# A hybrid decoder trunk on one core: another order of the weight folding and the x tiles in the prelude, the second block's rotary tables behind the softmax, and the third retention head scaled on the vector engine

## The chip, the cores and the metric

The kernel runs on one core of a Trainium2 chip. A core has a matrix engine (PE, with its weight loads shown as PEld), a vector engine (DVE), a scalar engine (ACT), a general engine (POOL) and an engine that mostly issues DMAs (SP). Each runs its own instructions in order, and waits on semaphores for the others. The metric is the time of one execution in microseconds (us) on the device; lower is better.

## The reference

One layer of a decoder trunk on x of 2048 tokens by 1024 columns, in f32, with 256 memory tokens. Cut to what matters:

```
h = rmsnorm(x, mix_norm_g)
q, k, v, g, u = split(h @ w_in)                  # 4 retention heads, pool
y_ret  = silu(g) * head_rmsnorm(retention(rope(q), rope(k), v), ret_gn_g)
y_pool = pool_mixer(u, pool_w, pool_scale)       # trailing windows 2, 4, 8, 16
x = x + concat([y_ret, y_pool]) @ w_out
mem_n = rmsnorm(mem, mem_norm_g)
k, v = split(mem_n @ wkv)                        # 4 heads of 256
p = softmax((rmsnorm(x, xa_norm_g) @ wq) @ k.T / 16)
x = x + (p @ v) @ wo
x = x + (silu(gate) * val) @ w_down              # gate, val: causal conv of rmsnorm(x) @ w_up
return rmsnorm(x, final_norm_g)
```

head_rmsnorm divides each head's row by its root mean square. rope rotates q and k by angles made from the token's position.

## The kernel before

Every f32 product is made of three matmuls in a reduced format: an operand is split into a high half (ACT copies it in that format, L257, or with a gain per row, L260) and a low half (DVE subtracts the high half, L241, or with the gain, L249); `passes` (L269 to L271) multiplies high by high, high by low and low by high. A matmul has 512 columns, in part of the prelude 256.

**The prelude**, `folded_weights`, folds the memory into the weights, so that attention needs neither q nor the values of the memory: it is a list of units, run in the order of one table. K0 to K7 are the memory's keys (weights `wkv` 0 to 7); V0 to V7 its values (`wkv` 8 to 15); M0 to M3 fold the transposed wq into the keys, one head each (two tiles of `wqT`), and store the result in Md; O0 to O3 fold `wo` into the values (two tiles of `wo` each) and store VWd; W0 to W3 fold the pool's weights into those of the output (`wout_p`) and store WPd. `pool_factors` loads `poolT` and prepares the pool's weights for W. A unit loads its weight tile of 128 x 1024 into a raw buffer, ACT and DVE split it into a buffer of `wides` (a high and a low half), and PE multiplies. There are nine raw buffers, in the tiles R, S and Z; a raw buffer comes free when its low half is done. `other_places` takes places out of `wides` and puts others in; the keys' own tile `kk` is one of these places.

Between the units, at the unit numbers in `x_at`, `load_x_wide` loads one of x's eight tiles of block 0 (`xT`, 128 x 1024) into a raw buffer, splits it into X with the norm's gain, squares it in place on ACT (L635) and adds it to `total` on DVE (`R<-R,Z` or `R<-R,S`); the raw buffer of that tile is free only after this addition. Of the two operations that make an x tile's halves and of the square and the sum, `keep_in_program_order` says that they stay where the code puts them. `rows_norm` makes the row norms from `total`, and `value_weights` loads and splits the weights for the values of the retention. Then `values` begins.

**A block** is 1024 of the 2048 tokens; two blocks follow one another (`b` = 0, 1). In each come the values, the heads' projections with the retention of four heads (h = 0 to 3, code in `retention`, in two halves `a` and `c` of four chunks each), the output projection with the residual, then the cross attention, and after both blocks the gated MLP. While PE works on one head's projections, ACT and DVE do the retention of the head before. In `retention`, `scaled` multiplies the head's result in PSUM, `aux`, by one factor for each row and chunk (`rr`), into `T`; it is ACT's, four operations of 128 columns for each half (L791). `mixed` then transposes it on PE (L796), and DVE applies gain and gate.

**The attention** (`attention`) goes through 16 score tiles (two head pairs, eight token tiles): 24 matmuls for a tile, then DVE's maximum (L899), ACT's exponentials (L903), DVE's reciprocal and scaling (L905, L245). The scaled tile is transposed on PE two tiles later (`turn`, L875). With the first tile, PE sums the squares of x (L350), and DVE makes the row norm from them. During the tiles, a generator `beside` is run one step at a time: in block 0 it is `stored_tables(1)`, which makes the sines and cosines of block 1's positions. It loads the positions (L647), and its first operation on DVE turns them into angles (L245, `T<-T,consts`). What is left of `beside` is run after the last tile.

The order of instructions on an engine is not that of the code alone: the tool that builds the program places instructions by when their inputs are expected, within what `keep_in_program_order` and `tc.issue_after(x)` allow; the latter lets what is issued inside it come only after the instruction x.

Of the kernel before, what the change touches and what calls it, by code (L numbers as in the profile page):

```python
# [12 lines left out]
ALU = mybir.AluOpType  # L13
AX = mybir.AxisListType

P = 128
# [4 lines left out]
T = 1024  # L21
SUB = 512
NB = SEQ // T
NS = T // SUB
HEADS = 4
# [111 lines left out]
def trunk(ctx, tc, xT, memT, pos, w_qkgu, w_v, wkv, wqT, wo, wout_r, wout_p, poolT, w_up, w_dn, vecs, consts, outT):  # L137
    nc = tc.nc
    pe, act, dve, pool, sp = nc.tensor, nc.scalar, nc.vector, nc.gpsimd, nc.sync
# [11 lines left out]
    G = cp.tile([P, 28 * T], F32R, tag="G", name="G")  # L151
# [18 lines left out]
    raws = Places([(R, j * T) for j in range(3)] + [(r, 0) for r in S], T)  # L170
# [69 lines left out]
    def tt(eng, out, a, b, op):  # L240
        return eng.tensor_tensor(out=out, in0=a, in1=b, op=op)  # L241

    def ts(eng, out, a, s1, op0, s2=None, op1=None):
        if op1 is None:
            return eng.tensor_scalar(out=out, in0=a, scalar1=s1, scalar2=None, op0=op0)  # L245
        return eng.tensor_scalar(out=out, in0=a, scalar1=s1, scalar2=s2, op0=op0, op1=op1)
# [4 lines left out]
    def bcast(v, n):  # L251
        return v.rearrange("p (a o) -> p a o", o=1).to_broadcast([P, v.shape[1], n])
# [55 lines left out]
    turned, chained = [], []  # L308
# [114 lines left out]
    def folded_weights():  # L423

        mp = B.take(4)
        mh = mp.r[:, : 2 * T].rearrange("p (k m) -> p k m", m=NMEM)
        ml = mp.r[:, 2 * T :].rearrange("p (k m) -> p k m", m=NMEM)
        kk, vv = B.take(4), B.take(4)
# [5 lines left out]
        def other_places(gone, places):  # L434
            for i in gone:
                wides.freed.remove(i)
            for at in places:
                wides.freed.append(len(wides.one))
                wides.one.append(Arena(*at[:2], 1, 2 * T))
# [24 lines left out]
        def row_pair(src):  # L464
            raw = new_raw()
            sp.dma_start(raw, src)
            return wide_pair(raw)

        u0 = wide()
        for k in range(KT):  # L470
            h, j = divmod(k, 4)
# [44 lines left out]
        def memory_values(n):  # L516

            project(KT + n)
            if n % 2:
                parted(vp4, n)  # L520
            if n == KT - 1:
                other_places((1, 2, 5, 6), [(G, mp.arena.base + (mp.first + i) * T) for i in (0, 2)])
                more.free()
                kk.free()

        def result():
            r = results.take()
# [27 lines left out]
        def output_weights(h):  # L555

            dp = [row_pair(wo[(2 * h + dt) * P : (2 * h + dt + 1) * P, :]) for dt in range(2)]
            for nh in range(2):
                t = result()
                for mt in range(2):  # L560
                    ps = mmps()
                    for dt in range(2):
                        lh = [vp4[:, 2 * h + dt, i, mt * P : (mt + 1) * P] for i in range(2)]
                        passes(ps, lh, [r[:, nh * SUB : (nh + 1) * SUB] for r in dp[dt]], dt == 0, dt == 1)
                    act.activation(tiles(t)[:, :, mt], ps.rearrange("p (n c) -> p n c", n=4), AF.Identity, scale=rn[:, mt : mt + 1])
                act.dma_start(VWd[4 * nh : 4 * nh + 4, :, 2 * h : 2 * h + 2].rearrange("n p k c -> p n (k c)"), t.rearrange("p (n d) -> p n d", n=4))
            if h == HEADS - 1:
                vv.free()

# [32 lines left out]

        K, V, M, O, W = keys, memory_values, score_weights, output_weights, pool_weights
        for f, *a in ((K, 0), (K, 1), (K, 2), (K, 3), (K, 4), (K, 5), (M, 0), (K, 6), (M, 1), (K, 7), (V, 0), (M, 2), (V, 1), (V, 2),
                      (M, 3), (V, 3), (O, 0), (V, 4), (V, 5), (O, 1), (V, 6), (O, 2), (V, 7), (W, 0), (W, 1), (O, 3), (W, 2), (W, 3),
                      (none_left,)):
            f(*a)
            if f is M and a[0] == 3:
                pool_factors()
            yield  # L610

# [122 lines left out]
    def retention(b, h, qkg, v):  # L734
# [10 lines left out]
        class Half:  # L745
# [41 lines left out]
                self.pr.free()  # L787

            def scaled(self, rr):
                for c in range(4):  # L790
                    act.activation(col(self.kn.f, c), col(self.y, c), AF.Identity, scale=rr[:, 4 * self.s + c : 4 * self.s + c + 1])  # L791

# [9 lines left out]
        a, c = Half(0), Half(1)  # L802
        both_ss, rr = small(8), small(8)
# [42 lines left out]
    def attention(sums, beside, pace):  # L846
# [41 lines left out]
        for i in range(2 * KT):  # L888
            hp, t = divmod(i, KT)
            ps = mmps()  # L890
            for k in range(KT):
                x2 = [X[:, 2 * k + j, t * P : (t + 1) * P] for j in range(2)]
                passes(ps, x2, mw[hp][k], k == 0, k == KT - 1)
            if i == 0:
                rn, _, _ = norm_tables(sums, wide=False)
                ts(dve, scl, rn, 1.0 / 16.0, ALU.mult)
                ts(dve, nscl, rn, -1.0 / 16.0, ALU.mult)
            mx, sm = small(2), small(2)
            dve.reduce_max(out=mx, in_=ps.rearrange("p (h m) -> p h m", h=2), axis=AX.X)  # L899
            ts(dve, mx, mx, nscl[:, t : t + 1], ALU.mult)  # L900
            e = TT.take()
            for j in range(2):
                act.activation(e.f[:, j * NMEM : (j + 1) * NMEM], ps[:, j * NMEM : (j + 1) * NMEM], AF.Exp,  # L903
                               bias=mx[:, j : j + 1], scale=scl[:, t : t + 1], accum_out=sm[:, j : j + 1])
            dve.reciprocal(sm, sm)  # L905
            for j in range(2):
                ej = e.f[:, j * NMEM : (j + 1) * NMEM]
                ts(dve, ej, ej, sm[:, j : j + 1], ALU.mult)
            if len(late) == 2:
                turn(*late.pop(0))  # L910
            late.append((prob[hp], t, e))
            if pace > 1 or i > 3:
                next(under[0], None)
            if i < KT - 2:
                next(more_m, None)
            else:
                for _ in range(pace):
                    next(beside, None)

        def end():  # L920
            for one in late:
# [1048 lines left out]
    under[0], spacing[0] = weight_sums(), 2  # L1970
    raws = Places([(R, j * T) for j in range(3)] + [(r, 0) for r in S] + [(Z.t, j * T) for j in range(4)], T)
    results = Places([(Z.t, j * T) for j in range(4, 8)], T)
    wv, total, x_at = [], raws.take(), (5, 7, 9, 10, 12, 13, 15, 17)
    for n, _ in enumerate(folded_weights()):
        if n in x_at:
            load_x_wide(x_at.index(n), total)
        if n == 21:
            rn = rows_norm([total])
        if n in (23, 24):
            wv.append(value_weights(len(wv), 0))  # L1980
        if n in (25, 26):
            wv.append(value_weights(len(wv), 1))
# [3 lines left out]
    raws = Places([(R, j * T) for j in range(3)] + [(r, 0) for r in S], T)  # L1986
    slow[0], paced[0], spacing[0] = False, True, 1
    for b in range(NB):
# [63 lines left out]
        beside = stored_tables(b + 1) if b + 1 < NB else first_tiles(own)  # L2052
        spacing[0] = (1, 2)[b]
        prob, behind[0] = attention(xs, beside, b + 1)
        spacing[0] = 4
        for _ in beside:
            pass
        under, paused = [iter(())], under
        Z = new_z(F32)
        xs = [TT.take() for _ in range(NS)]  # L2060
# [22 lines left out]
        for n in range(KT):  # L2083
# [9 lines left out]
            if n == KT - 1 and b + 1 < NB:  # L2093
                finish()
                wv = []
# [40 lines left out]
    raws = Places([(R, j * SUB) for j in range(6)] + [(r, j * SUB) for r in S for j in range(2)], SUB)  # L2136
# [114 lines left out]
```

## Time and profile before

| | us |
|---|---|
| median of 3 runs | 2420.11 (2417.14 to 2420.25) |
| the profiled execution | 2421.19 |
| its span, first to last instruction | 2419.4 |
| PE busy | 2392.6 |
| DVE busy | 1744.6 |
| ACT busy | 1336.2 |
| bytes moved by DMA | 513.10 MB, mean 212 GB/s |
| mean granted clock of PE | 0.997 of full |

The page has a part for each engine's busy time, the span in 40 slices, the DMA queues, the chain of work that ended last, and the costliest groups. In the other views, a row such as `L241 DVE TENSOR_TENSOR Z<-mm,T 128x512` names the line, the engine, the operation, what it writes and reads (buffer numbers left out) and the shape; `[3.60 <-ACT E L257]` behind a row says that the engine was idle for 3.60 us before it, and which instruction released it. The start times are us from the start of the span. The lines that the prediction rests on are shown with it.

### The profile page before, as it was taken

How to read it: one execution, taken by the hardware profiler on the slowest of the kernel's cores; microseconds unless marked ns; L12 is line 12 of the kernel's file. 1: busy time of each engine (PE TensorE's matmuls, PEld its weight loads, DVE VectorE, ACT ScalarE, POOL GpSimd, SP SyncE). 2: the span in 40 equal slices, each digit the busy share in tenths (PEclk: the TensorE clock that was granted, in tenths of full speed). 3: DMA queues.
4: the chain of work that ended last, by engine and by line, in shares of the span. 5: the costliest groups of instructions: out<-in, count | busy, mean ns of one | idle time of the engine just before them, and what ended most of it. 6: DMA issues, size and time to landing. Idle time of an engine off the chain costs nothing.

```text
span 2419.4 us, 33318 instructions
## 1 busy us (share of the span) xinstructions
PE 2392.6 (99%) x11232; PEld 2000.5 (83%) x11232; DVE 1744.6 (72%) x2889; ACT 1336.2 (55%) x2427; POOL 319.0 (13%) x484
## 2 busy tenths in 40 slices
PE   9899999999999999999999999999999999999998
PEld 9788888788888888888888888888888888888887
DVE  8687875655767764665788776887677698867876
ACT  6645554344444543344655555765555577666664
POOL 0066554552010000000000010010000000000000
PEclk9999999999999999999999999999999999999999
DMA  9999999989562244385568564765556479768952
GB/s 324 324 263 305 290 263 314 265 223 291 168 153 79 70 129 137 111 285 177 167 222 270 180 200 138 244 196 166 174 161 204 130 241 316 235 186 275 350 181 75
DMA packets 263468, 513.10 MB, mean 212 GB/s; under 512 B 29440, under 2 KB 50304, under 8 KB 263296
## 3 DMA queue, kind: packets, MB, share of 16 engines
q1 hardware_dynamic: 209776, 396.53, 49.9%
q0 software_dynamic: 37376, 86.00, 14.9%
q10 hardware_dynamic: 16144, 28.43, 3.2%
q8 instruction: 88, 1.44, 0.2%
q14 instruction: 84, 0.69, 0.1%
HBM read 408.62 MB, written 188.22 MB: 247 GB/s over the span
## 4 chain that ended last, share of the span: by engine, by line
PE 96%; DVE 2%; ACT 1%; DMA 1%; issue 0%; SPq 0%; DVEq 0%; ACTq 0%
PE mm L269 30%; PE mm L270 30%; PE mm L271 30%; PE aux L269 1%; PE aux L270 1%; PE aux L271 1%; DVE Z L241 1%; PE aux L755 1%; PE aux L875 1%; PE aux L781 1%; PE aux L766 1%; PE aux L783 1%; PE aux L350 0%; PE aux L757 0%; DMA S<-wkv 0%
## 5 line engine op out<-in xcount | busy, mean ns | idle before, releaser
L269 PE MATMUL mm<-G,Q 128*128 128x512 f32 (+1 forms) x1580 | 613.4, 388 | 6.1 <-ACT T L1681 3.1
L271 PE MATMUL mm<-G,Q 128*128 128x512 f32 (+1 forms) x1580 | 607.9, 387 | 0.2 <-DVE Q L241 0.2
L270 PE MATMUL mm<-G,Q 128*128 128x512 f32 (+1 forms) x1452 | 561.2, 387 | 0.2 <-DVE G L249 0.2
L270 PE MATMUL mm<-G,E 128*128 128x512 f32 (+1 forms) x1124 | 429.4, 382 | 0.0
L271 PE MATMUL mm<-G,E 128*128 128x512 f32 (+1 forms) x1124 | 427.4, 382 | 1.2 <-DVE E L241 1.2
L269 PE MATMUL mm<-G,E 128*128 128x512 f32 (+1 forms) x1124 | 427.9, 383 | 0.0
L269 PEld LDWEIGHTS mm<-G,Q 128*128 128x128 f32 x1580 | 296.9, 188 | 67.3 <-ACT T L1681 3.6
L271 PEld LDWEIGHTS mm<-G,Q 128*128 128x128 f32 x1580 | 296.8, 188 | 59.9 <-DVE Q L241 0.4
L270 PEld LDWEIGHTS mm<-G,Q 128*128 128x128 f32 x1452 | 272.9, 188 | 54.1 <-DVE G L249 0.4
L241 DVE TENSOR_TENSOR Z<-Z,mm 128x512 f32<-128x512 f32 (+1 forms) x322 | 215.4, 673 | 120.3 <-PE mm L271 113.8
L249 DVE SCALAR_TENSOR_TENSOR Z<-Z,vecs 128x1024 f32<-128x1024 f32 x176 | 224.7, 1280 | 50.2 <-ACT Z L1113 46.8
L271 PEld LDWEIGHTS mm<-G,E 128*128 128x128 f32 x1124 | 211.3, 188 | 42.6 <-DVE E L241 1.6
L270 PEld LDWEIGHTS mm<-G,E 128*128 128x128 f32 x1124 | 211.3, 188 | 41.0
L269 PEld LDWEIGHTS mm<-G,E 128*128 128x128 f32 x1124 | 211.3, 188 | 40.9
L1050 ACT ACTIVATE E<-R 128x512 fp32r<-128x512 f32 (+1 forms) x165 | 101.4, 615 | 140.9 <-PE mm L270 132.2
L241 DVE TENSOR_TENSOR T<-T 128x512 f32<-128x512 f32 (+4 forms) x196 | 134.2, 689 | 18.3 <-ACT T L416 11.2
L241 DVE TENSOR_TENSOR Q<-R,Q 128x512 fp32r<-128x512 f32 x152 | 105.1, 694 | 53.5 <-ACT Q L257 30.5
L1113 ACT ACTIVATE Z<-Z,vecs 128x1024 f32<-128x1024 f32 x88 | 109.1, 1241 | 38.1 <-DVE Z L241 37.2
L997 ACT ACTIVATE G<-T 128x512 fp32r<-128x512 f32 x180 | 108.4, 623 | 37.6 <-DMA T<-Gd 28.1
L1050 ACT ACTIVATE E<-S 128x512 fp32r<-128x512 f32 (+1 forms) x107 | 65.8, 615 | 104.9 <-PE mm L270 101.6
L241 DVE TENSOR_TENSOR E<-R,E 128x512 fp32r<-128x512 f32 (+2 forms) x126 | 84.9, 676 | 43.7 <-ACT E L1050 41.8
L1050 ACT ACTIVATE Q<-R 128x512 fp32r<-128x512 f32 (+1 forms) x123 | 75.5, 614 | 55.5 <-PE mm L270 46.5
(349 smaller groups left out, 4070.7 us busy)
## 6 DMA issues: line engine op xcount, KB each, us to landing
T<-Gd SPq DMA_DIRECT2D x168, 256.0 KB, 4.3
Ud<-w_up POOLq DMA_DIRECT2D x132, 256.0 KB, 9.9
Gd<-Z SPq DMA_DIRECT2D x110, 256.0 KB, 2.7
R<-Ud SPq DMA_DIRECT2D x106, 256.0 KB, 2.7
R<-w_up SPq DMA_DIRECT2D x80, 256.0 KB, 3.1
S<-Ud SPq DMA_DIRECT2D x70, 256.0 KB, 2.7
Gd<-T SPq DMA_DIRECT2D x56, 256.0 KB, 3.4
T<-Xd SPq DMA_DIRECT2D x53, 256.0 KB, 4.1
```

The source lines that it names most:

```text
L241: return eng.tensor_tensor(out=out, in0=a, in1=b, op=op)
L249: return dve.scalar_tensor_tensor(out=out, in0=a, scalar=s, in1=b, op0=op0, op1=op1)
L269: pe.matmul(ps, lh, rh, start=start, stop=False, skip_group_check=more)
L270: pe.matmul(ps, lh, rl, start=False, stop=False, skip_group_check=more)
L271: latest[0] = pe.matmul(ps, ll, rh, start=False, stop=stop, skip_group_check=more)
L755: pe.matmul(col(sc, c), self.ch(k, c), self.ch(q, c), start=True, stop=True)
L766: pe.matmul(col(kv, c), col(self.kn.f, c), self.ch(v, c, h * T), start=True, stop=True)
L781: pe.matmul(col(y, c), col(self.pr.f, c), self.ch(v, c, h * T), start=True, stop=self.cur[c] is None)
L783: pe.matmul(col(y, c), self.ch(q, c), self.cur[c], start=False, stop=True)
L997: one = act.activation(hi, x, AF.Copy, scale=-1.0 if i == 2 else 1.0)
L1050: act.activation(p2[:, 0, :w], self.raw[i].f[:, :w], AF.Copy)
L1113: act.activation(self.c[g].f, a[:, 2:], AF.Identity, bias=cb[:, f : f + 1], scale=cw[2][:, f : f + 1])
```

## The change

The change does three things, and has no other parts.

1. In the prelude the table of units is changed from V4 on: W0 to W3 stand among V4 to V7 and O1 to O3, not at the end; O2 follows V7. `pool_factors` comes after M2, not M3. x's tiles are issued at the units 5, 8, 10, 13, 16, 18, 19, 21 in place of 5, 7, 9, 10, 12, 13, 15, 17, so the last four come four or more units later; the row norms follow unit 24 rather than 21, the first value weights units 22 and 23. The keys' tile `kk` leaves `wides` and is freed after O1, not after V7.
2. In the attention the steps of `beside` may come only after the scaling of the score tile at hand, and those left at the end only after the last transpose's evacuation.
3. The third head (h = 2) of each block has its two halves scaled by DVE, one operation of 512 columns each, in place of ACT's four of 128 columns.

```diff
@@ memory_values
-                other_places((1, 2, 5, 6), [(G, mp.arena.base + (mp.first + i) * T) for i in (0, 2)])
+                other_places((1, 2), [(G, mp.arena.base + (mp.first + i) * T) for i in (0, 2)])
                 more.free()
-                kk.free()
@@ output_weights
+            if h == 1:
+                other_places((5, 6), [])
+                kk.free()
@@ folded_weights
-                      (M, 3), (V, 3), (O, 0), (V, 4), (V, 5), (O, 1), (V, 6), (O, 2), (V, 7), (W, 0), (W, 1), (O, 3), (W, 2), (W, 3),
+                      (M, 3), (V, 3), (O, 0), (W, 0), (V, 4), (V, 5), (W, 1), (O, 1), (V, 6), (W, 2), (V, 7), (O, 2), (W, 3), (O, 3),
-            if f is M and a[0] == 3:
+            if f is M and a[0] == 2:
                 pool_factors()
@@ retention
             def scaled(self, rr):
+                if h == HEADS - 2:
+                    tt(dve, four(self.kn.f[:, :SUB]), four(self.y), bcast(rr[:, 4 * self.s : 4 * self.s + 4], P), ALU.mult)
+                    return
                 for c in range(4):
@@ attention
-                ts(dve, ej, ej, sm[:, j : j + 1], ALU.mult)
+                scaled = ts(dve, ej, ej, sm[:, j : j + 1], ALU.mult)
...
-                for _ in range(pace):
-                    next(beside, None)
+                with tc.issue_after(scaled.ins):
+                    for _ in range(pace):
+                        next(beside, None)
@@ the calls
-    wv, total, x_at = [], raws.take(), (5, 7, 9, 10, 12, 13, 15, 17)
+    wv, total, x_at = [], raws.take(), (5, 8, 10, 13, 16, 18, 19, 21)
-        if n == 21:
+        if n == 24:
             rn = rows_norm([total])
-        if n in (23, 24):
+        if n in (22, 23):
             wv.append(value_weights(len(wv), 0))
...
-        for _ in beside:
-            pass
+        with tc.issue_after(turned[-1].ins):
+            for _ in beside:
+                pass
```

Three places show how this moves instructions. The first is SP in the prelude, the loads that end with those of O0 and V4: `wo` are the weights of the O units, `wkv` here those of V, `wqT` those of M, `xT` tiles of x; Z, R and S on the left are raw buffers. Before:

```order
L466 DMA R<-wqT 128x1024
L576 DMA R<-poolT 128x4x128
L466 DMA Z_74<-wo 128x1024
L633 DMA Z_74<-xT 128x1024
L340 DMA R<-wkv 128x1024
L633 DMA Z_74<-xT 128x1024
L466 DMA S_79<-wqT 128x1024
L466 DMA R<-wo 128x1024 x2
L340 DMA S_79<-wkv 128x1024
L466 DMA Z_74<-wo 128x1024
```

and in the changed kernel, from the same `poolT` on:

```order
L578 DMA R<-poolT 128x4x128
L340 DMA Z_74<-wkv 128x1024
L466 DMA R<-wqT 128x1024
L466 DMA Z_74<-wqT 128x1024
L340 DMA S_79<-wkv 128x1024
L466 DMA R<-wo 128x1024 x2
L635 DMA Z_74<-xT 128x1024
L340 DMA Z_74<-wkv 128x1024
L635 DMA Z_74<-xT 128x1024
L466 DMA S_78<-wqT 128x1024
```

Of the first block's rows of `wo`, the one behind `poolT` is tile 1, the row of two is tiles 2 and 3, those of O1, and the last row is tile 0, which O0 needs first; seven x tiles are loaded ahead of it. In the changed order both tiles of O0 come in one row, ahead of the fourth x tile to be loaded; the `wkv` row behind that x tile is `wkv` 10, the weights of V2, which before had been issued ahead of these rows.

The second place is DVE at the beginning of block 0's attention; `sm<-aux` begins the row norm from PE's sums, L899 (L904 in the changed kernel) is the first tile's maximum. Before:

```order
L241 TENSOR_TENSOR T<-T,aux_3947 128x512
L245 TENSOR_SCALAR T<-T,consts 128x512
L246 TENSOR_SCALAR sm_4009<-aux_4000 128x8
L246 TENSOR_SCALAR T<-T 128x512
L246 TENSOR_SCALAR sm_4010<-sm_4009 128x8
L241 TENSOR_TENSOR T<-T 128x512
L241 TENSOR_TENSOR sm_4012<-sm_4010 128x8
L899 TENSOR_REDUCE sm_4026<-mm_3974 128x2
```

and in the changed kernel:

```order
L241 TENSOR_TENSOR T<-T,aux_3941 128x512
L246 TENSOR_SCALAR sm_4003<-aux_3994 128x8
L246 TENSOR_SCALAR sm_4004<-sm_4003 128x8
L241 TENSOR_TENSOR sm_4006<-sm_4004 128x8
L904 TENSOR_REDUCE sm_4020<-mm_3968 128x2
```

The tables' first operation, `T<-T,consts`, stood ahead of the row norm and is gone from here; it now stands some 50 rows later, behind the scaling of a later score tile.

The third place is ACT at the third head of block 0; `aux` is the head's result, L1681 (L1687 in the changed kernel) evacuates a projection's bank, L257 splits an operand. Before:

```order
L964 ACTIVATE halo<-consts 128x2
L791 ACTIVATE T<-aux_2751,sm_2649 128x128 x4
L791 ACTIVATE T<-aux_2763,sm_2649 128x128 x4
L964 ACTIVATE halo<-consts 128x2
L257 ACTIVATE G<-Z_74 128x512 x2
L1681 ACTIVATE T<-mm_3054 128x512
```

and in the changed kernel, first ACT's rows:

```order
L1672 ACTIVATE Q<-R 128x512
L970 ACTIVATE halo<-consts 128x2
L257 ACTIVATE G<-Z_74 128x512 x2
L1687 ACTIVATE T<-mm_3048 128x512
L1703 ACTIVATE R<-mm_2874 64x512 x2
```

and then DVE's:

```order
L245 TENSOR_SCALAR sm_2649<-sm_2649,consts 128x8
L241 TENSOR_TENSOR T<-aux_2751,sm_2649 128x512
L241 TENSOR_TENSOR T<-aux_2763,sm_2649 128x512
L241 TENSOR_TENSOR R<-R,Z_74 128x512
L241 TENSOR_TENSOR Z_74<-Z_74 128x512
```

The two scalings stand on DVE right behind the factor that they need, ahead of the pool's windows (`R<-R,Z`, `Z<-Z`), and ACT goes from the splits to the evacuation with nothing of the head between.

## The prediction

> **What bounds the kernel now.** I read the page first, parts 1 and 4.
>
> ```profile
> PE 2392.6 (99%) x11232; PEld 2000.5 (83%) x11232; DVE 1744.6 (72%) x2889; ACT 1336.2 (55%) x2427; POOL 319.0 (13%) x484
> ...
> PE 96%; DVE 2%; ACT 1%; DMA 1%; issue 0%; SPq 0%; DVEq 0%; ACTq 0%
> ```
>
> PE is the bound: 99% busy, 96% of the chain that ended last. The diff neither adds nor removes a matmul, so it can gain only what PE loses by waiting, or by a lower clock behind a wait. So next comes the view of waits, for PE alone (engine and operation that waited, what released it, us in total, times, longest).
>
> ```profile
> PE mm L269 <- ACT E L257: 3.6, 1, 3.6
> PE aux L875 <- DVE T L245: 3.4, 1, 3.4
> PE mm L269 <- ACT T L1681: 3.1, 2, 1.9
> PE mm L269 <- ACT Q L257: 2.7, 3, 1.5
> ...
> PE mm L269 <- ACT Z L592: 1.1, 1, 1.1
> ```
>
> The waits are few and single. The windows of 20 us tell where PE is short (columns: sum; busy time of PE, PEld, DVE, ACT, POOL; granted clock; DMA share; GB/s).
>
> ```profile
> 0.00:20.00 20.00, 16.76 (x108) 15.37 (x109) 13.98 (x26) 14.45 (x22) 0.20 (x4) 1.00 0.93 324
> 20.00:40.00 20.00, 20.00 (x169) 20.00 (x168) 18.23 (x34) 13.81 (x17) 0.00 (x0) 1.00 0.94 349
> 40.00:60.00 20.00, 20.00 (x169) 20.00 (x168) 20.00 (x24) 12.71 (x15) 0.00 (x0) 1.00 0.88 299
> 60.00:80.00 20.00, 16.11 (x91) 14.09 (x90) 17.73 (x18) 13.57 (x16) 0.00 (x0) 0.83 1.03 378
> ...
> 100.00:120.00 20.00, 17.40 (x91) 14.14 (x90) 15.19 (x30) 14.50 (x22) 0.00 (x0) 1.00 0.96 315
> ...
> 460.00:480.00 20.00, 16.64 (x73) 13.33 (x72) 19.08 (x53) 10.42 (x27) 13.70 (x21) 0.91 0.99 229
> ```
>
> Two of them lose clock as well: 60 to 80 (0.83) and 460 to 480 (0.91). DVE is full from 40 to 60, just ahead of the largest wait.
>
> **The prelude's order.** The timeline around the largest wait, the start of O0:
>
> ```profile
> 52.39 1.22 DVE L241 TENSOR_TENSOR R<-R,S 128x1024 f32<-128x1024 f32 x1
> ...
> 61.78 2.55 DVE L241 TENSOR_TENSOR R<-R,Z 128x1024 f32<-128x1024 f32 x2
> ...
> 63.02 0.33 SPq L466 DMA_DIRECT2D Z<-wo  x1
> ...
> 70.15 1.04 ACT L257 ACTIVATE E<-Z 128x1024 fp32r<-128x1024 f32 x1
> ...
> 71.24 2.07 PE L269 MATMUL mm<-E,G 128*128 128x512 f32 x4 [3.60 <-ACT E L257]
> ...
> 74.03 0.80 PE L270 MATMUL mm<-E,G 128*128 128x512 f32 x1 [0.29 <-DVE E L241]
> ...
> 75.05 0.63 PE L269 MATMUL mm<-E,G 128*128 128x512 f32 x1
> ```
>
> Followed back: PE waits 3.60 us for the split of wo's first tile; that waits for its load, and the load was issued at 63.02 only, because its raw buffer was that of x tile 4 and came free when DVE had added that tile to the sum of squares (61.78, first of two). DVE was late since by then it had seven x tiles to serve. The price of this stop: 3.60, then 0.29, then matmuls of 0.63 us at half clock. A window's clock is a mean over its busy time, so the clock cost 16.11 x (1 - 0.83) = 2.7. Together **6.6 us**.
>
> The change has four x tiles ahead of O0, not seven. What one tile costs, from the groups of 40 to 80 us, kept apart by shape:
>
> ```profile
> L249 DVE SCALAR_TENSOR_TENSOR G<-Z,vecs,G 128x1024 fp32r<-128x1024 f32 x4 | 5.1, 1275 | 0.0
> L241 DVE TENSOR_TENSOR R<-R,Z 128x1024 f32<-128x1024 f32 x4 | 4.9, 1220 | 0.1
> L260 ACT ACTIVATE G<-Z,vecs 128x1024 fp32r<-128x1024 f32 x4 | 4.6, 1143 | 0.6 <-DMA Z<-xT 0.6
> L635 ACT ACTIVATE Z<-Z 128x1024 f32<-128x1024 f32 x4 | 4.1, 1042 | 0.0
> ```
>
> Three tiles less are 3 x (1.28 + 1.22) = 7.5 us of DVE, 3 x (1.14 + 1.04) = 6.5 us of ACT and 1.5 MB of loads taken from a stretch where DVE is full; they come back behind O0. In SP's new order both of O0's weight loads stand ahead of x4, and neither takes an x tile's buffer. I take the 6.6 us as gone.
>
> What is late next: wkv10, the weights of V2. SP issued them early before; now they stand behind x4's load, in the buffer of x tile 1, which comes free with DVE's add of that tile. In the changed DVE order that add ends 2.8 us of work sooner than the add that began at 52.39 before, so at 50.7 if DVE never waits, 52.5 with two short waits. PE gets to V2 after 397 matmuls; 277 lie before 40.00 by the windows, 169 in the next 20 us, so 40 + 120 x 20 / 169 = 54.2. The load's duration, from the DMA view of 0 to 125 us (KB each, median us to landing):
>
> ```profile
> Z<-wkv SPq DMA_DIRECT2D x10, 512.0 KB, 7.2
> ...
> R<-wqT SPq DMA_DIRECT2D x2, 512.0 KB, 4.3
> ```
>
> So it lands between 55.0 and 59.7, its split ends 1.04 later, and PE waits between 1.8 and 6.6 us. I take **+3.5**, near the short load, as few loads are outstanding while SP itself waits for buffers. Later, W0 to W3 are spread among V and O units. Before they stood at the end, where PE waited 1.5 (Q L257) and 1.1 (Z L592, the evacuation of a W unit behind its store). I take both as gone, **-2.6**; if the new stores collide in the same way, nothing is gained. From O1 to V7 there are now three split buffers instead of five. A matmul of 256 columns takes 20 / 169 = 0.12 us, so PE spends 2.8 us on the one buffer of a V unit (24 matmuls), 5.7 on the two of an O unit (24 of twice the width), 1.4 on the one of a W unit (6 of these). DVE and ACT refill a buffer in 1.22 + 1.04 = 2.3 us. V and O units have slack, W units owe 0.9 each and stand between them, so I cost this at nothing, with W's debt of 4 x 0.9 = 3.6 us if that cover is gone, and give the case that DVE as a whole becomes late to a rival. Prelude: -6.6 + 3.5 - 2.6 = **-5.7**, bounds -9.2 and +7.5 (the DVE work moved, if nothing hides it).
>
> **Tables behind the softmax.**
>
> ```profile
> 449.24 1.84 PE L350 MATMUL aux<-consts,T 128*128 128x1 f32 x16
> 449.51 1.15 SPq L647 DMA_DIRECT2D T<-pos  x2
> ...
> 458.95 0.49 DVE L245 TENSOR_SCALAR T<-T,consts 128x512 f32<-128x512 int32 x1 [14.76 <-PE mm L271]
> 459.35 0.16 DVE L246 TENSOR_SCALAR sm<-aux 128x8 f32<-128x8 f32 x1
> ...
> 465.07 0.61 DVE L245 TENSOR_SCALAR T<-T,sm 128x256 f32<-128x256 f32 x2
> ...
> 465.48 0.91 PE L875 MATMUL aux<-consts,T 128*128 128x128 f32 x4 [3.36 <-DVE T L245]
> ```
>
> The sums that the norm needs were ready at 451.1, yet DVE idled 14.76 us, since the first operation of block 1's tables stood ahead of it and waited for positions issued at 449.51. (The releaser named, PE, had long been done; it was the load.) With the norm first, the 5.7 us from 459.35 to 465.07 run from 451.1 to 456.8; PE wants the result at 465.48 - 3.36 = 462.1. The wait goes with some 5 us to spare, and with it 16.64 x (1 - 0.91) = 1.5 of clock: **-4.9**, bounds -4.9 and 0. The tables themselves (DVE products, sines on ACT, loads by SP) are taken from the stretch 460 to 480, where DVE is full (19.08), and now run beside later score tiles and behind the last turn, where there is room:
>
> ```profile
> 520.00:540.00 20.00, 20.00 (x96) 16.50 (x95) 9.22 (x22) 7.46 (x22) 14.58 (x23) 1.00 1.08 259
> ```
>
> If that cover failed, a late turn would wait about as long as the first did, 3.4 and 1.5 us.
>
> [...] Waits of 3.60 and 3.36 us were followed by half clock; those of 1.5 and 1.1 were not (100 to 120 has clock 1.00). [...]
>
> **Third head.**
>
> ```profile
> 325.91 2.15 ACT L791 ACTIVATE T<-aux,sm 128x128 f32<-128x128 f32 x8
> ...
> 328.00 1.19 ACT L257 ACTIVATE G<-Z 128x512 fp32r<-128x512 f32 x2
> ...
> 329.04 0.64 ACT L1681 ACTIVATE T<-mm 128x512 f32<-128x512 f32 x1
> ...
> 329.73 0.50 PE L269 MATMUL mm<-G,Q 128*128 128x512 f32 x1 [1.29 <-ACT T L1681]
> ...
> 845.41 0.50 PE L269 MATMUL mm<-G,Q 128*128 128x512 f32 x1 [1.86 <-ACT T L1681]
> ```
>
> ACT runs without a gap from the eight scalings to the evacuation that PE waits for, in both blocks. Without the eight, 2.15 us, each wait can go: at most 1.29 + 1.86 = 3.15. Two DVE products take their place, whose cost the trace brackets by a DVE evacuation of that shape:
>
> ```profile
> L241 DVE TENSOR_TENSOR Z<-mm,T 128x512 f32<-128x512 f32 x12 | 7.9, 682 | 0.8 <-PE mm L271 0.8
> ```
>
> 1.4 us on a DVE that is nearly full there; the low half of the next operand comes from it. I take **-2.5**, bounds -3.15 and +0.5. [...]
>
> **Sum.** -5.7 - 4.9 - 2.5 = -13.1 on the profiled run of 2421.19 (its span, 2419.4, and 1.8 around it): 2408.1. That run lies 1.1 above the median shown, 2420.11; in the median's terms **2407**.
>
> **Rivals.** *Half clock at V2*: the load takes its median, the wait is 6.6 and costs 2.7 of clock, 9.3 in place of 3.5: -7.3, 2413. For it: the load is bound to a busy DVE. Against: DMA is the less loaded at 40 to 60. *The tables only move their wait* to the last turn, attention 0: -8.2, 2412. *The prelude gives its gain back*: the x tiles, 7.5 us later, delay the first values by as much as O0 gains; prelude 0, third head between 0 and -2.5: 2413 to 2415. *Changed, but not as told*: DVE takes ACT's place in front of the evacuation at the third head; -10.6, 2409.5. *Slower*: DVE becomes the bound of the prelude's second half. What it idles from 60 to 120 is the window less its busy time:
>
> ```profile
> 60.00:120.00 60.00, 53.51 (x304) 46.32 (x303) 41.55 (x57) 41.60 (x57) 0.00 (x0) 0.94 0.93 324
> ```
>
> 60.00 - 41.55 = 18.4 us. If it keeps that idle time, because with three buffers it waits for PE and PE for it, 7.5 us more work ends 7.5 later, and the stop at V2 with half clock (9.3) comes ahead of it: +16.8 - 4.9 - 2.5 = +9.4, 2429.5. It decides from a prelude that loses over 7.4 us. Against it: 18.4 is more than twice 7.5.
>
> **How the numbers follow.** Forecast 0.52 (its own range 2402 to 2411), half clock 0.12, wait moved 0.08, not as told 0.06, gain given back 0.15, slower 0.07. A measurement of this kernel tells some 0.2%, 4.8 us, from no change: faster is below 2415.3. The given-back case lies at that edge, and I count a third of it as faster, the rest as the same; of the slower case 0.01 stays within. So 0.82 faster, 0.12 the same, 0.06 slower, with rounding. The low end takes every bound: -9.2 - 4.9 - 3.15 and some 2 us of waits too small to be listed, 2401; the high end holds the given-back case without a gain at the third head and 2 us of new small waits, 2417.
>
> **What would show it.** Right: no wait of 3 us by O0, clock 1.00 in 460 to 480, no wait for L1681's successor above 0.5, one wait for E L257 near 55 us, values starting 4 to 8 us sooner. Wrong: a DVE near full from 80 to 110 with PE waiting for it, a clock below 0.95 between 40 and 60, a wait at the last turns of block 0's attention.

## The result, and the profile after

The changed kernel takes **2425.49 us**, the median of 14 runs (2422.25 to 2429.08). The kernel before took 2419.89 on the same chip, also 14 runs. The ratio is 1.0022, 95% interval 1.0013 to 1.0030: it is slower, by 3 to 7 us. The prediction was 2407, and its range ended at 2417.

Two rows fix where that happened: the first and the last matmul of the heads' scores (L781, in the changed kernel L783). They divide the span into the prelude with the values, the two blocks up to the last head, and the rest. Timeline of PE, before:

```profile
227.18 0.61 PE L781 MATMUL aux<-Z,T 128*128 128x128 f32 x4
...
873.70 0.39 PE L781 MATMUL aux<-Z,T 128*128 128x128 f32 x2
```

and after:

```profile
237.45 0.61 PE L783 MATMUL aux<-Z,T 128*128 128x128 f32 x4
...
876.67 0.39 PE L783 MATMUL aux<-Z,T 128*128 128x128 f32 x2
```

The first part became 10.3 longer. The second became 7.3 shorter (646.5 to 639.2), near the 4.9 + 2.5 that the tables and the third head were to bring. The rest became 1.4 longer. So the loss lies in the prelude. (The first of the two rows is the start of the heads; its time is called the **mark** below.)

The waits of PE after, the view that began the prediction:

```profile
PE mm L269 <- ACT Z L594: 6.2, 2, 5.9
PE mm L271 <- DVE Q L241: 4.3, 1, 4.3
PE mm L269 <- ACT E L257: 2.5, 1, 2.5
PE mm L269 <- ACT Q L257: 1.1, 2, 0.9
...
PE mm L269 <- DVE T L241: 1.0, 1, 1.0
PE mm L269 <- ACT S L1672: 0.7, 1, 0.7
PE mm L269 <- ACT T L1687: 0.5, 2, 0.3
```

The stop of 3.6 by O0 and the 3.4 at L875 (now L880) are gone, and the waits for the evacuation L1681 (now L1687) fell from 3.1 to 0.5. Two new stops stand on top. The windows tell where (busy PE, PEld, DVE, ACT, POOL; clock; DMA share; GB/s):

```profile
60.00:80.00 20.00, 20.00 (x139) 18.44 (x139) 15.83 (x17) 15.28 (x19) 0.00 (x0) 1.00 0.88 318
80.00:100.00 20.00, 19.68 (x124) 17.21 (x122) 16.09 (x15) 14.98 (x20) 0.00 (x0) 1.00 1.01 371
100.00:120.00 20.00, 14.12 (x64) 11.87 (x65) 12.26 (x28) 12.43 (x20) 0.00 (x0) 0.83 0.70 243
160.00:180.00 20.00, 15.02 (x57) 11.30 (x56) 15.47 (x26) 12.08 (x26) 14.45 (x19) 0.91 1.02 270
...
460.00:480.00 20.00, 20.00 (x99) 16.70 (x99) 14.53 (x44) 9.94 (x26) 10.89 (x18) 1.00 1.06 300
```

60 to 80 and 460 to 480 are whole now. 100 to 120 and 160 to 180 are not, and both lost clock as well. The prediction took a window's clock as a mean over PE's busy time; it is a mean over the window's whole time. In the trace's own clock record the first of these windows has one stretch at half clock, 6.83 us from 102.02 on, and (20 - 6.83 / 2) / 20 is the 0.83 shown. But PE runs again only from 105.89 on:

```profile
105.89:108.84 2.95, 2.95 (x7) 2.37 (x8) 2.44 (x3) 2.81 (x4) 0.00 (x0) 0.50 0.16 52
```

So the clock costs it 2.95 / 2 = 1.5 us there. In the other window the stretch lasts 3.41 us from 170.28 on, all of it in PE's work, and costs 1.7.

**The first new stop.** ACT's timeline after, 82 to 124 us:

```profile
87.03 0.37 ACTq L596 DMA_DIRECT2D WPd<-Z  x1
...
87.52 0.86 ACTq L596 DMA_DIRECT2D WPd<-Z  x1
...
95.29 0.40 ACTq L565 DMA_DIRECT2D VWd<-Z  x1
...
103.79 0.37 ACTq L565 DMA_DIRECT2D VWd<-Z  x1
104.20 1.15 ACT L260 ACTIVATE G<-Z,vecs 128x1024 fp32r<-128x1024 f32 x1 [6.32 <-DMA WPd<-Z]
```

The units here run in the order W1, O1, V6, W2, so these are O1's two stores into VWd; the expectations of e12 and e13 below call them O2's by mistake. The second stood in ACT's queue until 103.79, everything of ACT behind it for 6.32 us, and PE ran dry at W2:

```profile
105.89 0.79 PE L269 MATMUL mm<-Q,G 128*128 128x512 f32 x1 [5.91 <-ACT Z L594]
```

What was waited for, from the chain of work that ended last:

```profile
87.52 16.20 DMA WPd<-Z
103.79 0.37 ACTq L565
```

W1's second store took 16.20 us from its issue to its landing (the last signal of its end in the trace, at 103.71), and the VWd store started at 103.79. The tile view of WPd gives the four stores' times to landing, min, median and max. Before:

```profile
DMA to landing us min/median/max: 4.8/5.7/6.7
```

After:

```profile
DMA to landing us min/median/max: 8.5/11.1/16.2
```

The VWd store writes another table from another buffer, so the data explain no wait. The program does: as built, it has each of the 1,504 DMAs of SP's and ACT's queues signal its end on one of eight semaphores, given out in the order of the program, and has a DMA's issue wait until the one eight places ahead has ended. Four DMAs of the changed program, with their places in that order (place, engine, line, tile written, its semaphore):

```
63 ACT L596 WPd  6
64 ACT L596 WPd  7
...
71 SP  L712 w_v  6
72 ACT L565 VWd  7
```

The trace records each DMA's semaphore and bears this out. W1's first store lands at 99.71, and the `w_v` load, which has its semaphore next, starts at 99.77; the second lands at 103.71, and the VWd store starts at 103.79. In none of the fifteen traces does a DMA of these two queues start before the one ahead of it on the same semaphore has landed, in 1,496 pairs each before and after and some 1,490 in each of the others.

**The second new stop** is 4.26 us at 170.05, with 0.72 and 0.97 behind it at 177.22 and 193.13:

```profile
170.05 0.62 PE L271 MATMUL mm<-G,Q 128*128 128x512 f32 x1 [4.26 <-DVE Q L241]
```

PE waits for the low half of a tile of `w_qkgu`; DVE made the like at 153.98 before and at 169.31 now. Backwards: SP issued that load at 154.97 (before 143.24), since a raw buffer came free late, since the second sum of the pool ran late, and its first operation on ACT, before:

```profile
121.33 0.73 ACT L1543 ACTIVATE T<-R,vecs 128x512 f32<-128x512 f32 x1 [1.36 <-issue]
```

started ten us later after the change, behind the evacuations of O3, which is the last unit now:

```profile
129.08 1.84 ACT L564 ACTIVATE Z<-mm,rnm 128x512 f32<-128x512 f32 x3 [5.37 <-PE mm L271]
130.81 0.70 ACT L564 ACTIVATE Z<-mm,rnm 128x512 f32<-128x512 f32 x1
131.95 0.75 ACT L1549 ACTIVATE T<-R,vecs 128x512 f32<-128x512 f32 x1
```

DVE stood idle until then:

```profile
132.73 0.69 DVE L241 TENSOR_TENSOR R<-R 128x512 f32<-128x512 f32 x1 [10.47 <-ACT T L1549]
```

Whether O3's place is the cause, or its weights and the pool's loads are late through the first stop, this trace alone doesn't say.

### The profile page after: what moved, and what is told of

It is laid out like the page before. It is cut to its first block, busy times and chain, and to the rows that moved or that the text cites. A ratio compares the mean times of both kernels' runs of the same rounds, so it can differ in the third digit from the quotient of the medians.

```text
span 2423.8 us, 33301 instructions
## 1 busy us (share of the span) xinstructions
PE 2395.6 (99%) x11232; PEld 2001.3 (83%) x11232; DVE 1750.1 (72%) x2893; ACT 1331.8 (55%) x2410; POOL 309.8 (13%) x484
## 4 chain that ended last, share of the span: by engine, by line
PE 95%; DVE 2%; DMA 2%; ACT 1%; issue 0%; SPq 0%; ACTq 0%; DVEq 0%
PE mm L269 30%; PE mm L271 29%; PE mm L270 29%; PE aux L269 1%; PE aux L270 1%; DMA WPd<-Z 1%; PE aux L271 1%; PE aux L783 1%; PE aux L757 1%; PE aux L768 1%; PE aux L880 1%; PE aux L785 1%; PE aux L350 0%; DVE Z L241 0%; DVE T L241 0%
```

## The experiments

Ratios are to runs of the kernel before on the same chip, with 95% intervals.

**The three parts apart.** The kernel before with two parts or one. Each part's diff is the change's own; e1 leaves out all that concerns units, `x_at` and places, e2 has that alone, e3 only `scaled`, e5 only the two `issue_after`.

> The kernel before with the tables behind the softmax and the third head on DVE, without the prelude's part. Theory A (the prelude alone is what costs; the other two gain what the trace of the changed kernel suggests, about 5 us in block 0's attention and 1.3 + 1.6 at the third heads): 7 to 9 us faster than before, 2411 to 2413; no wait for L245 by the first turn, clock 1.00 there. Rival B (one of the two small parts also costs somewhere, so that the three together lose): between 3 faster and 3 slower.

> The kernel before with the prelude's part alone. Theory A: 11 to 15 us slower than before, 2431 to 2435, with the three waits of the changed kernel again: about 2.5 us for wkv's split near 59, about 6 us behind W's store near 106, about 4 us for DVE's low half near 170. Rival B (the loss comes from the parts together): within 6 us of before, without one of these waits.

> The kernel before with the third head scaled by DVE alone. Theory A: the two waits for L1681 (1.29 and 1.86) shrink to about 0.3 each, 2 to 3 us faster. Rival: DVE, nearly full there, hands the wait on; within 1 us of before.

> The kernel before with the tables behind the softmax alone. Theory A: the wait of 3.4 us by the first turn goes with its half clock, 4 to 5 us faster than before in the trace between 450 and 480, and 2 to 5 us in the median (the wait's size differs from run to run). Rival B: the tables come too late at the attention's end; a wait of over 1 us at a turn between 520 and 570, gain under 1.

| run | us, median (runs) | ratio to before |
|---|---|---|
| e1, tables and third head | 2416.78 (11) | 0.9979, 0.9970 to 0.9988 |
| e2, prelude alone | 2431.91 (5) | 1.0051, 1.0039 to 1.0064 |
| e3, third head alone | 2418.34 (11) | 0.9989, 0.9980 to 0.9998 |
| e5, tables alone | 2419.93 (11) | 0.9997, 0.9989 to 1.0006 |

The prelude alone costs 9 to 15 us and has both stops of its own. PE's waits in e2:

```profile
PE mm L269 <- ACT Z L594: 6.1, 2, 5.8
PE aux L877 <- DVE T L245: 3.6, 1, 3.6
PE mm L271 <- DVE Q L241: 3.5, 1, 3.5
```

The third head brings 2.9 us by the medians, 2.5 foreseen. The tables bring less than the trace promised: their wait is gone in e5 too, but its medians differ by 0.6 us, interval -2.7 to +1.5. From mark to last head e5 gained 2.8 (228.21 to 871.89) and e1, with both parts, 6.6 (228.61 to 868.49). Together they are -4.4 us by the medians, -2.9 to -7.3, where 7 to 9 had been expected. Part of what e5 lost can be seen. It keeps the second block's wait for the third head, 1.87 us at 842.06, and after it runs 3.41 us at half clock, which costs 1.7. In the kernel before the same wait, 1.86 at 845.41, left the clock whole; the last section comes back to this.

**W's stores off ACT's queue.** The changed kernel, with POOL's queue for WPd:

```diff
-                    act.dma_start(WPd[...], ...)
+                    nc.gpsimd.dma_start(WPd[...], ...)
```

> The changed kernel with the four stores of the W units (WPd) issued by POOL, which is idle in the prelude, in place of ACT; SP's, DVE's and PE's orders are the same. Theory C (the store itself takes 16 us and need not hurt; what hurts is that ACT's next store but one is not issued before it, and all of ACT stands behind that): the wait of 5.9 near 106 falls below 1 us and its half clock goes, 6 to 9 us faster than the changed kernel, 2416 to 2420; whether the wait near 170 goes too tells if it is a consequence. Rival D (the DMA engines are full there, so that the wait only moves to the next evacuation, which needs the store's buffer): less than 2 us faster than the changed kernel.

2420.39 us, 11 runs, ratio 0.9998 (0.9989 to 1.0007): 5 us better than the changed kernel, just short of theory C's 6 to 9. The stop of 5.9 is gone and the clock from 100 to 120 is 1.00, while the second stop is as before. Waits of PE in e4:

```profile
PE mm L271 <- DVE Q L241: 4.3, 1, 4.3
PE mm L269 <- ACT E L257: 2.5, 1, 2.5
PE mm L269 <- ACT Q L257: 1.6, 2, 1.0
```

So the first stop comes from ACT standing behind those stores, and the second is not its consequence.

**The last units, and each half of the prelude's change.** e6 is e4 with O3 ahead of W3. In e6 O3's results take the buffers in which W2's half of the last two stores stands, so W2's quarter of WPd isn't the reference's; the work is the same. e7 is the changed kernel with the old table of units, e8 with the old places of the x tiles.

```diff
# e6, on top of e4
-(O, 2), (W, 3), (O, 3)
+(O, 2), (O, 3), (W, 3)
# e7: the changed kernel's table of units as before
# e8
-x_at = (5, 8, 10, 13, 16, 18, 19, 21)
+x_at = (5, 7, 9, 10, 12, 13, 15, 17)
```

> The kernel with W's stores on POOL (the run before) and O3 and W3 swapped at the end of the table. Theory E (the wait of 4.3 us at the first head's projections comes from O3 as the last unit: its weights are loaded last, its four evacuations and two of the values stand on ACT ahead of the first operation of the pool's sums, and so DVE reaches the splits of w_qkgu late): ACT's first L1549 runs some 8 us sooner, the waits of 4.3, 0.7 and 1.0 shrink to under 1.5 together, 4 to 6 us faster than with the queue alone, 2414 to 2417. Rival F (w_qkgu's loads are late by themselves): a wait of over 3 us stays.

> The changed kernel with the old table of units, but x's tiles later. Theory G (later x tiles are good, the order of W and O is what costs): no wait over 2 us at O0, none of 5.9 behind W's store, none of 4.3 at the first head; the wait of 2.5 for wkv near 59 stays; 3 to 6 us faster than the run without the prelude's part, 2411 to 2414. Rival H (the x tiles late make DVE the bound before the values): slower than that run.

> The changed kernel with x's tiles at their old units, but the new table of units. Theory G: the wait at O0 is back (about 4 us and half clock), the one for wkv near 59 is gone; W's stores stand in a stretch with fewer loads, so that they land in under 10 us and the wait behind them is under 3 us; 2418 to 2426. Rival H: the wait behind W's store stays near 6.

| run | us, median (11 runs each) | ratio to before | mark |
|---|---|---|---|
| e6 | 2415.45 | 0.9977, 0.9968 to 0.9986 | 226.42 |
| e7 | 2414.20 | 0.9977, 0.9968 to 0.9986 | 226.54 |
| e8 | 2415.74 | 0.9981, 0.9972 to 0.9990 | 226.66 |

e6 has lost the second stop with nothing but the swap: in this order of the x tiles, O3 as the last unit makes it. And neither half of the prelude's change, alone, costs anything: only together do they lose. Nor does either half alone show a gain. e7 and e8 carry the tables and the third head too, so the run to hold them against is e1, whose 0.9979 (0.9970 to 0.9988) can't be told from 0.9977 and 0.9981; for e7, 3 to 6 us better than e1 had been expected. In e7 the W units stand at the end again and their stores land in 4.1 to 8.1 us.

e8 came out better than expected, 2415.74 against 2418 to 2426. The wait at O0 did not come back, though the x tiles are loaded as in the kernel before. W's stores come 3 us later than in the changed kernel and take 8.0 to 12.1 us. O1's second VWd store again stands eight places behind a store of W, but behind the first, which had landed at 101.68, before the VWd store's own data were ready at 102.11, so nothing waited. O3 is last there too (the pool's first sum begins at 124.88, as late as the 125.25 of e4), yet PE comes to the place of the second stop 4.3 us later than in e4 (162.1 against 157.8), and DVE has the operand 4.4 us sooner (158.3 against 162.7). PE had been held up at V2 and at M3:

```profile
58.72 0.58 PE L269 MATMUL mm<-G,E 128*128 128x256 f32 x1 [2.56 <-ACT E L257]
61.47 0.58 PE L269 MATMUL mm<-G,E 128*128 128x256 f32 x1 [1.96 <-ACT E L257]
```

**O3 earlier, x tile 1 earlier.** e9 and e10 put O3 ahead of W3 with W2 between, so that all of WPd is made (e10 with W's stores on POOL's queue); e11 is e7 with x tile 1 one unit earlier, for the wait at V2.

```diff
# e9, e10
-(V, 6), (W, 2), (V, 7), (O, 2), (W, 3), (O, 3)
+(V, 6), (V, 7), (O, 2), (W, 2), (O, 3), (W, 3)
# e11, on top of e7
-x_at = (5, 8, 10, 13, 16, 18, 19, 21)
+x_at = (5, 7, 10, 13, 16, 18, 19, 21)
```

> The changed kernel with its last units in the order V6, V7, O2, W2, O3, W3: O3 is no longer the last, the W units stay spread, W's stores stay on ACT's queue. Theory A (O3 as the last unit, with wo's last tiles loaded late, holds ACT's evacuations, with them the first sum of the second pool, the buffers of w_qkgu and the operand that PE waits for near 170 us): the waits of 4.3, 0.7 and 1.0 us between 160 and 200 us go, the clock there is 1.00, the stop of about 6 us behind W's slow store stays: about 2420, 5 below the changed kernel. Rival B (the x tiles, loaded later, make the pool's sum late by themselves): a wait of 3 to 4 us stays near 170, 2424 to 2426.

> As the run before, with W's stores issued by POOL's queue. Theory A with the theory on the store (ACT stands in order behind a store that waits for another's end): both stops are gone, 2415 to 2416, as in the run with the swapped units, here with all of W's tables whole. Rival B: the wait near 170 stays, about 2420.

> The changed kernel with the old table of units and x tile 1 one unit earlier (x_at begins 5, 7 in place of 5, 8). Theory: the wait of 2.46 us near 59 us is that of wkv10's load for the buffer of x tile 1; one unit earlier the buffer comes free about 2 us earlier, the wait goes or falls below 1 us and the clock of 60 to 80 is 1.00: 2411 to 2413, against 2414.2 with 5, 8. Rival: DVE's work up to there sets it, whichever tile stands ahead: the wait stays or moves to the next load, 2414 to 2416.

| run | us, median (runs) | ratio to before | mark |
|---|---|---|---|
| e9 | 2411.29 (5) | 0.9962, 0.9950 to 0.9975 | 223.09 |
| e10 | 2413.88 (6) | 0.9969, 0.9957 to 0.9981 | 225.91 |
| e11 | 2410.29 (5) | 0.9955, 0.9942 to 0.9967 | 222.01 |

e9 is 9 us better than theory A had it: the second stop went as foreseen (the pool's first sum begins at 117.41), but the first went as well, although W's stores stay on ACT's queue and take up to 14.4 us. The program again has the reason: here O1's second VWd store stands eight places behind the first of W's two stores, not the slow second; that one landed at 97.39, and the VWd store's data were ready only at 97.63. Moving the stores to POOL gained nothing more: e10's mark is later than e9's, though its 2413.88 is below the 2415 to 2416 expected. In e11 the wait of 2.46 for V2 is gone, as foreseen, and no wait of PE is above 1.1 us.

**One place on in the round of eight.** One load of `w_v` is split in two, so that every later DMA has the next semaphore; PE's order is the same.

```diff
-        sp.dma_start(raw, w_v[2 * kp : 2 * kp + 2])
+        for i in range(2):        # for kp = 1 only
+            sp.dma_start(raw[:, i * SUB : (i + 1) * SUB], w_v[2 * kp + i])
```

> The changed kernel with one 512 KB load of w_v (the second) split into two of 256 KB; PE's order is the same, of ACT's and DVE's one split stands one place earlier. Every DMA of SP's and ACT's queues ends on one of eight completion semaphores, handed round in the order of the program, and waits first for the DMA eight places ahead. In the changed kernel the second VWd store of O2 stands eight places behind W's slow second store; with one more load between them it stands eight places behind a load of wo. Theory: the stop of 5.9 us with its half clock goes as it did when W's stores left ACT's queue, the waits near 170 us (4.3, 0.7, 1.0) stay: about 2420. Rival (the slow store holds ACT because of the full DMA engines or of its buffer, whichever semaphore it has): the stop stays, 2425.

2425.06 us, 11 runs, ratio 1.0014 (1.0005 to 1.0023): the number was wrong, the mechanism is seen all the better. I had overlooked that O1's first VWd store, 71st now, stands eight places behind W's first store, which is slow too. ACT's timeline of e12:

```profile
87.96 0.37 ACTq L596 DMA_DIRECT2D WPd<-Z  x1
...
88.45 1.43 ACTq L596 DMA_DIRECT2D WPd<-Z  x1
...
101.19 0.37 ACTq L565 DMA_DIRECT2D VWd<-Z  x1
101.66 1.06 ACT L257 ACTIVATE G<-Z 128x1024 fp32r<-128x1024 f32 x1 [4.02 <-DMA WPd<-Z]
101.73 0.52 ACTq L565 DMA_DIRECT2D VWd<-Z  x1
```

W's first store landed at 101.11; O1's first VWd store waited until 101.19, and the second, whose place now lies behind a load of wo, followed at once. The place behind W's second store, which took 16.7 us and so landed at 105.16, belongs to a load of `w_v` on SP, and SP stood until just then:

```profile
105.22 4.36 SPq L716 DMA_DIRECT2D Z<-w_v  x2
```

Neither the data nor the buffer of a `w_v` load has to do with WPd. So it is the shared semaphore that hands the slow store's delay to whoever has its place: ACT stops for 4.02 us instead of 6.32, PE for 3.39 instead of 5.91. What is gained there is lost behind, where PE now waits 4.72 with a clock of 0.83 (160 to 180).

**Both repairs.** e9's units with e11's x tiles.

> The units in the order V6, V7, O2, W2, O3, W3 of the run with O3 earlier, and x tile 1 one unit earlier (x_at begins 5, 7). In its program the second VWd store of O2 stands eight places behind a load of wo, not behind a store of W. Theory: neither stop is there, and the wait of 2.5 us near 59 us for wkv10 is gone too: 2408 to 2410, at or below the 2410.3 of the old table with 5, 7. Rival (the W units among the V and O units cost in small waits what the stops' absence gains): 2411 to 2413.

**2409.11 us**, 5 runs, ratio 0.9953 (0.9940 to 0.9966), mark 221.84, as expected: better than both kernels, by 12 us and 16. The waits of PE:

```profile
PE mm L269 <- ACT Q L257: 2.2, 3, 1.0
PE mm L271 <- DVE E L241: 1.2, 2, 0.9
PE mm L450 <- DVE T L214: 1.1, 1, 1.1
```

e13 and e11 can't be told apart by these runs; they are 2 and 3 us from the 2407 that the change itself missed.

## Why the prediction was wrong

Step by step:

- **O0's stop, -6.6: right.** Gone in the changed kernel with its half clock (60 to 80 now 1.00), and in every run that has the new x tiles. It is gone in e8 too, with the old x tiles and the new units, so fewer x tiles ahead of O0 are not the only way to lose it.
- **V2, +3.5: right in mechanism, and near in size partly by luck.** One wait of 2.46 at 59.37, for E L257 as named. e11 shows that in this order it hangs on x tile 1's buffer. But the load was issued at 53.52, over 1 us later than worked out, it took 3.9 us and not 4.3 to 7.2, its split stood behind two others on ACT until 58.27, and PE came at 56.9, not at 54.2; these misses nearly cancel. That such a stop costs no clock was the author's estimate: it held here, where 2.46 us left 1.00 in 60 to 80, and not in e12, where 2.51 us at the same place was followed by 0.92.
- **W among the other units, -2.6: the step that failed.** The prediction took W's old waits as gone and wrote "if the new stores collide in the same way, nothing is gained", a bound of zero. It never asked what else is in flight there: SP issues ten loads of 512 KB between 82.59 and 95.44, three of them of x, DMA is full (1.01), and a store takes 16.20 us where it took 6.7 at most. Nor did it name what is queued behind that store. The price was 5.91 + 1.5 of clock = 7.4 us. e4 shows it for ACT's queue, e12 for the semaphore. That the load on the DMA engines is what stretched the store is read from the windows and not tested by itself, and it can't be the whole cause: in e4, with the DMA as full (1.01 from 80 to 100), the same two stores on POOL's queue took 8.5 and 10.1 us.
- **O3 as the last unit: not priced at all.** The text counted split buffers from O1 to V7 and "W's debt" of 3.6, but not what follows the last unit: O3's evacuations stand on ACT ahead of the pool's first sum, and two engines further on PE waits 4.26 + 0.72 + 0.97, with 1.7 of clock: 7.7 us. e6 and e9 show it.
- Sum of the prelude: gone 6.6 + 1.5 + 1.1, new 2.46 + 7.4 + 7.7, net +8.4, against -5.7 forecast; the mark moved by 8.8 to 10.3 (the unchanged prelude reaches it at 227.18 to 228.61 in four profiles). With both mistakes undone and the wait at V2 still there, e9's mark is 4.1 to 5.5 sooner: the forecast -5.7 was that of a prelude in which nothing new collides. e13, without that wait, is 5.3 to 6.8 sooner, where the same terms without the 3.5 would give 9.2.
- **Tables, -4.9, third head, -2.5: the mechanisms right, the tables' size too large.** In the changed kernel's profile both waits are gone, 7.3 from mark to last head, the clock of 460 to 480 whole, L1687 with 0.5 of waits. By medians the two bring less: 4.4 in e1, and 5.1 as what the change costs less than its prelude alone (5.6 against 10.7). The third head keeps its 2.5, so it is the tables: e5's interval excludes -4.9. In e5's trace some 1.5 us of the gain are lost again between the second block's first scores (738.19, before 741.54) and its last (871.89, before 873.70): the 1.7 at half clock behind the third head's wait. The rest stays open.
- Of the rivals, "slower" had the sign and the place, not the mechanism: DVE was to be the bound, but it has 12.26 of 20 us in the worst window and waits there itself. "Gives its gain back" allowed for delayed values; the values' first evacuation came 3.8 us sooner (123.02 against 126.78), almost the 4 to 8 named as a sign of being right, but that was no gain: PE had taken these values ahead of O3 and had done some 25 matmuls less by then. The second evacuation came 0.5 later (131.38 against 130.90). The loss came in two single stops.
- Of the 4.4 us between the two spans, 0.9 lie in the last eight matmuls and have nothing to do with the change, as the end of this text shows.

## What to carry to other kernels

When a store or a load is moved to another stretch, its own duration there has to be estimated anew from what else is in flight (W's store took 6.7 us at most before, 16.20 after), and then everything that stands behind it: its engine's queue (ACT stood for 6.32 us), and, where a program hands its completion semaphores round as this one does, the DMA that is given the same one next, on whichever engine (in e12 the `w_v` load on SP, until 105.22). When the order of a list is changed, price the successor of the new last item, not only the items. Two halves of a change that cost nothing alone can lose together, so it pays to time them apart, each against the kernel that has all the rest.

## What was not expected of the hardware

A wait shorter than 3 us was sometimes followed by a lower clock and sometimes not, while the prediction put no clock on the 3.5 us that it expected at V2. The wait there of 2.46 us left 1.00 in 60 to 80 in the changed kernel; in e12, the same wait at the same place, 2.51 us,

```profile
58.90 0.39 PE L269 MATMUL mm<-G,E 128*128 128x256 f32 x1 [2.51 <-ACT E L257]
```

was followed by

```profile
60.00:80.00 20.00, 20.00 (x129) 18.54 (x129) 15.35 (x16) 14.21 (x18) 0.00 (x0) 0.92 0.88 299
```

The profile's record of the granted clock tells the two cases apart. Between 14 us and the last matmuls its stretches at half clock are 69.89 to 76.72 and 465.84 to 469.25 before, 102.02 to 108.84 and 170.28 to 173.70 after: 3.41 us or twice that. The two starts of one trace lie 116 times 3.413 us apart before and 20 times after. So the span is counted below in steps of 3.413 us that go through these starts; the first whole step begins 1.62 us into the span before and 3.03 after. The wait at the second block's third head fell into one step in e5, in which PE idled 1.87 us, and the next step ran at half clock:

```profile
839.45:842.86 3.41, 1.54 (x11) 1.18 (x9) 3.41 (x6) 2.48 (x5) 0.00 (x0) 1.00 0.26 77
842.86:846.27 3.41, 3.41 (x10) 2.63 (x9) 1.30 (x3) 0.00 (x0) 0.00 (x0) 0.50 0.24 74
```

In the kernel before the same wait fell into two steps, 1.16 and 0.69 us, and neither was followed by half clock:

```profile
841.30:844.72 3.42, 2.25 (x15) 1.73 (x13) 2.72 (x5) 3.35 (x8) 0.00 (x0) 1.00 0.11 29
844.72:848.10 3.38, 2.69 (x12) 2.21 (x13) 2.79 (x5) 0.64 (x2) 0.00 (x0) 1.00 0.20 56
```

The wait at V2 fell into two steps in the changed kernel, 0.73 and 1.73 us, and whole into one in e12. The kernels before and after have 16 steps at full clock between 14 and 2395 us in which PE idled for over 0.6 us: the 12 with 0.61 to 1.73 us were followed by full clock, the 4 with 2.05 to 3.18 us by half clock. Over all fifteen traces, the 62 with at most 1.83 us were followed by full clock and the 19 with 1.87 us or more by half clock. One stretch at half clock is left over, at 92.50 in e8 (0.91 in 80 to 100): it follows a step without such a wait; most of that step is sixteen matmuls of one column. So in these traces the clock after a wait went with how much of it fell into one step, not with its length, and the steps did not lie at the same place in every run.

The last matmuls of the program show the same: eight of one group, behind a wait of 0.29, before:

```profile
2409.58 1.16 PE L1325 MATMUL mm<-consts,sm 128*128 128x128 f32 x8 [0.29 <-DVE sm L249]
```

and after:

```profile
2413.02 2.08 PE L1331 MATMUL mm<-consts,sm 128*128 128x128 f32 x8 [0.28 <-DVE sm L249]
```

Nothing in the change touches them. After, half clock begins at 2412.84, just ahead of them; before, only at 2414.85, behind them. The profiles of the experiments have the one or the other duration (1.16 in e5, e11 and e13, 2.07 in e3, e9 and e12). So one us of a difference between two single profiles of this kernel can come from the last ten us alone; medians of several runs are needed below that.
